# Weight-sum jobs of the pooling layer moved to earlier steps, and rows for the norm loaded ahead of the second half of transposed x

## The chip, the cores and the metric

The kernel runs on one core of one Trainium2 chip. The metric is the device time of one execution in microseconds (us), the median of several executions. Matrix products run on TensorE (PE in the profile), elementwise work on VectorE (DVE), ScalarE (ACT) and GpSimd (POOL); SyncE (SP) issues most loads, POOL issues the stores to DRAM scratch.

## The reference

Two layers, each `h = h + Mixer(rms_norm(h))`, and a norm at the end, for 1024 tokens of width 1024, in fp32. Layer 0 is the pooling mixer, layer 1 stick-breaking attention. The change touches only layer 0:

```python
def pooling_mixer(u, w_in, w_group, scale, w_out):
    proj = u @ w_in                                   # 1024 x 4096
    xb, z = jnp.split(proj, 2, axis=-1)
    xg = xb.reshape(B, S, N_POOL_GROUPS, POOL_GROUP_DIM)
    pooled = jnp.stack(
        [causal_pool_minus_self(xg[:, :, gi], w) for gi, w in enumerate(POOL_WINDOWS)],   # 2, 4, 8, 16
        axis=2)
    mixed = jnp.einsum('bsgi,gio->bsgo', pooled, w_group).reshape(B, S, D_INNER)
    y = mixed * scale * jax.nn.silu(z)
    return y @ w_out
```

## The kernel before

Every product is made of three matmuls in a fast 32-bit type: each operand is split into a high part (ACT, lines 98, 158, 161) and a low part (DVE, lines 99, 159, 162), and high-high, high-low and low-high are added up (`mm3`, lines 89 to 91). A matmul has 512 columns. The first 480 us of the trace are layer 0, the rest is layer 1, which the change leaves alone.

The input projection and the output projection go by a scheme of Strassen's kind: seven products of half blocks in place of eight, for which sums of blocks of the weights and of the activations are formed first.

**The first product (lines 343 to 381).** Tokens are handled in two halves. `c1` is the first product of four blocks of the projection with the one half of transposed x (32 loads and splits in `first_w` and `load_xt`, 96 matmuls), `c2` the same blocks with the other half (`load_xt(k, 1, ...)`, splits into `g4_*` and `g3_*`, 96 matmuls). x isn't scaled for the norm when it is multiplied; the factor is applied afterwards. `factors(l)` (line 176) loads four tiles of rows of x for half `l`, squares and sums them on ACT (line 182) and raises the mean to the power of -1/2 on POOL (184, 185). `spread(l)` (187) has PE copy these factors along the partitions (line 191, four matmuls of 128 columns) and ACT bring them to SBUF (193). `to_u(k, l)` (195) multiplies a tile of x by them on DVE, eight times a half. In `factors` the tiles for the rows come from the two buffers each of `wsum` and `xb`, so the rows for the second half wait until those of the first have been squared.

**The rest of the projection.** `Group(c).rest` (line 244) is what is left of one group of blocks: it loads four blocks of the weights into `a_raw` (6 buffers), has POOL form sums of them (`sums`, lines 221 to 223, and 276), splits blocks and sums (98, 99) and runs 84 matmuls, and DVE brings the products together (214, 250, 260, 266, 269). The order of the blocks is such that the splits of the sums wait for line 223.

**The loop over the four window groups (line 417, `gi`).** In each: two steps `cp`, each a Group (numbers 4 gi and 4 gi + 2) and then `pool_block` for two blocks: sums over the window by repeated adds on DVE (294, two adds for a window of 4, four for 16, on rows of about 1024), 296, 297, and splits into `pl` (302, 303); then two steps `op`, each a Group for the gate (16 + 4 gi, 18 + 4 gi), and `mixed` for two blocks: products of the pooled blocks (PE starts them once all `pl` of the four blocks are there), line 314 on DVE, and POOL stores and differences for the output projection (321 to 338). The first group of both kinds is that of `c1` and `c2`.

**The weight-sum jobs.** The output projection needs sums of blocks of its weights too. `out_sums(kb)` (226) forms those of one of eight parts: four loads on SP into the same `a_raw` buffers, four adds on POOL (221, 222, 223, 231) and four stores that POOL issues (233). The results are read only after the loop. Before, jobs stand after the Group of these steps: 1 at `gi` 0, `op` 1; 2 and 3 at `gi` 1, `op` 0 and 1; 0, 4 and 5 at `gi` 2, `cp` 0, `op` 0 and 1; 7 and 6 at `gi` 3, `cp` 0 and `op` 0.

**What sets the order.** Instructions are emitted in the order of the code; a scheduler places them on each engine by its own timeline, with the release of tile buffers as a constraint, and each engine then works its list in order. A job that is emitted at one step is thus mixed with the sums of the Group behind it, and pool buffers tie the loads to the work that frees them.

Of the kernel before, what the change touches and what calls it, by code (L numbers as in the profile page):

```python
# [9 lines left out]
F32 = mybir.dt.float32  # L10
# [5 lines left out]
P = 128  # L16
S = 1024
D = 1024
DI = 2048
NT = S // P  # L20
NK = D // P
# [24 lines left out]
def trunk(ctx, tc, x, xt, g, pw, pg, psc, pwo, sqk, sv, sz, swo, nf, out):  # L46
# [55 lines left out]
    def raw_of(src, pool, name="w_raw", **kw):  # L102
        raw = pool.tile([P, 512], F32, name=name, **kw)
        nc.sync.dma_start(raw, src)
        return raw
# [31 lines left out]
    def bank():  # L137
        return banks.tile([P, 512], F32, name="bk")

    with tc.tile_pool(name="l0", bufs=2) as l0:  # L140
# [3 lines left out]
        def u_tile(n, kb):  # L144
            t = tuple(l0.tile([P, 512], F32R, name=f"g{n}_{kb}{x_}", bufs=1) for x_ in "hl")
            G[n][kb] = t
            return t

        def pl_tile(dtype=F32):
            return l0.tile([P, 512], dtype, name="pl", bufs=16)  # L150

        def wide(i):
            return l0.tile([P, S + 16], F32, name="xb" if i % 2 else "wsum")

        def split_to(t, raw, scale=None):
            hi, lo = t
            if scale is None:
                act(hi, raw, AF.Copy)
                nc.vector.tensor_tensor(lo, raw, hi, ALU.subtract)
            else:  # L160
                act(hi, raw, AF.Copy, scale=scale)
                nc.vector.scalar_tensor_tensor(lo, in0=raw, scalar=scale, in1=hi, op0=ALU.mult, op1=ALU.subtract)

        def load_xt(k, l, n):


            j, kb = divmod(k, 4)
            t = B[j, l, kb] = pl_tile()
            nc.sync.dma_start(t, xt[k * P:(k + 1) * P, HALVES[l] * 512:HALVES[l] * 512 + 512])
            split_to(u_tile(n, kb), t, g_sb[:, k:k + 1])  # L170
# [5 lines left out]
        def factors(l):  # L176

            ssq = small.tile([P, 4], F32, name="ssq4")
            for j in range(4):
                t = wide(j)[:, :D]  # L180
                nc.sync.dma_start(t, xv[4 * HALVES[l] + j])
                act(t, t, AF.Square, accum_out=ssq[:, j:j + 1])
            rs = rss[l] = small.tile([P, 4], F32, name="rs4")
            nc.gpsimd.tensor_scalar(rs, ssq, 1.0 / D, EPS, ALU.mult, ALU.add)
            nc.gpsimd.tensor_tensor(rs, rs, mhalf.broadcast_to([P, 4]), ALU.pow)

        def spread(l):

            pt = bank()
            for j in range(4):  # L190
                nc.tensor.transpose(pt[:, j * P:(j + 1) * P], rss[l][:, j:j + 1].broadcast_to([P, P]), ident)
            rsb[l] = l0.tile([P, 512], F32, name="w_raw" if l else "rsb", bufs=3 if l else 1)
            act(rsb[l], pt, AF.Copy)
# [7 lines left out]
        def u_split(n, kb, raw):  # L201
            split_to(u_tile(n, kb), raw)
# [15 lines left out]
        def sums(a11, a21, a22):  # L218

            s1 = l0.tile([P, 512], F32, name="w_raw", bufs=3)  # L220
            nc.gpsimd.tensor_tensor(s1, a21, a22, ALU.add)
            nc.gpsimd.tensor_tensor(a21, a21, a11, ALU.add)
            nc.gpsimd.tensor_tensor(a11, a11, s1, ALU.add)
            return s1

        def out_sums(kb):

            a = {(i, j): raw_of(pwo[8 * j + kb][:, i * 512:i * 512 + 512], l0, "a_raw", bufs=6)
                 for i in range(2) for j in range(2)}
            s1 = sums(a[0, 0], a[1, 0], a[1, 1])  # L230
            nc.gpsimd.tensor_tensor(a[0, 1], a[0, 1], a[0, 0], ALU.add)
            for n, t in (5, s1), (7, a[1, 0]), (6, a[0, 0]), (3, a[0, 1]):
                nc.gpsimd.dma_start(wd[n][kb], t)
# [48 lines left out]
        def xb_tile(name="xb", bufs=2):  # L282
            t = l0.tile([P, S + 16], F32, name=name, bufs=bufs)
            nc.gpsimd.memset(t[:, S:], 0.0)
            return t

        def pool_block(gi, c, xb, pooled):
            w = WINDOWS[gi]
            cur, d = xb, 1
            while d < w:  # L290
                nxt = l0.tile([P, S + 16], F32, name="wsum")
                n = S + 16 - 2 * d + 1 if 2 * d < w else S
                n = min(n, S + 16 - d)
                nc.vector.tensor_tensor(nxt[:, :n], cur[:, :n], cur[:, d:d + n], ALU.add)  # L294
                cur, d = nxt, 2 * d
            nc.vector.tensor_tensor(cur[:, S - w + 1:S], cur[:, S - w + 1:S], ratio[w], ALU.mult)
            nc.vector.scalar_tensor_tensor(  # L297
                cur[:, :S], in0=cur[:, :S], scalar=1.0 / w, in1=xb[:, :S], op0=ALU.mult, op1=ALU.subtract)
            for half in range(2):
                cs = slice(half * 512, half * 512 + 512)  # L300
                hi, lo = pooled[c, half] = pl_tile(F32R), pl_tile(F32R)
                act(hi, cur[:, cs], AF.Copy)
                nc.vector.tensor_tensor(lo, cur[:, cs], hi, ALU.subtract)
# [41 lines left out]
        def first_w(j):  # L345
            for a, c in enumerate(first):
                for i in range(2):
                    raw = raw_of(pw[c + i][:, j * 512:j * 512 + 512], l0, "a_raw", bufs=6)
                    n = (7, 5)[a]
                    t = fw[a, i, j] = tuple(  # L350
                        l0.tile([P, 512], F32R, name=f"g{n}_{2 * i + j}{x_}", bufs=1) for x_ in "hl")
                    split_to(t, raw)
                    if j == 0:
                        load_xt(2 * a + i, 0, 1)
                    else:
                        load_xt(4 + 2 * a + i, 0, 2)

        def first_mm(ps, a, i, k, n):
            wh, wl = fw[a, i, k // 4]
            ks = slice(k % 4 * P, k % 4 * P + P)  # L360
            mm3(ps, wh[:, ks], wl[:, ks], *G[n[k // 4]][k % 4], k == 0, k == NK - 1)

        c1 = {(a, i): bank() for a in range(2) for i in range(2)}
        for j in range(2):
            first_w(j)
            for k in range(4 * j, 4 * j + 4):
                for a, i in c1:
                    first_mm(c1[a, i], a, i, k, (1, 2))
        factors(0)
        factors(1)  # L370
        for k in range(NK):
            load_xt(k, 1, (4, 3)[k // 4])
        spread(0)
        c2 = {}
        for a in range(2):
            for i in range(2):
# [12 lines left out]
        for kb in range(4):  # L389
# [5 lines left out]
            dve(B[0, 1, kb], B[0, 0, kb], B[0, 1, kb], ALU.subtract)  # L395
            dve(B[0, 0, kb], t3[kb], B[0, 0, kb], ALU.add)
            u_split(6, kb, B[0, 0, kb])
        firsts = [[xb_tile() for _ in range(2)], [l0.tile([P, S], F32, name="t0") for _ in range(2)]]
        fns = AF.Copy, AF.Silu
        for i in range(2):  # L400
            scaled(firsts[1][i], c1[1, i], 0, fns[1])
# [12 lines left out]
        for kb in range(4):  # L414
            u_split(3, kb, B[1, 1, kb])

        for gi in range(len(WINDOWS)):
            pooled = {}
            for cp in range(2):
                if gi + cp:  # L420
                    dst = [xb_tile("old" if gi == 0 and i else "xb", 2 - (gi == 0 and i)) for i in range(2)]
                    Group(gi * 4 + 2 * cp).rest(dst, AF.Copy)
                    if gi > 1 and cp == 0:
                        out_sums((0, 7)[gi - 2])
                else:
                    dst = firsts[0]
                for i in range(2):
                    pool_block(gi, 2 * cp + i, dst[i], pooled)
            for op in range(2):
                if gi == 3 and op == 1:  # L430

                    y1 = []
                    for kb in range(4):
                        t = wide(kb)
                        raw, hi = t[:, :512], t[:, 512:S].bitcast(F32R)
                        nc.sync.dma_start(raw, yd[1][kb])
                        split_to((hi, raw.bitcast(F32R)), raw)
                        y1.append((hi, raw.bitcast(F32R)))
                if gi + op:
                    dst = [l0.tile([P, S], F32, name="t0") for _ in range(2)]  # L440
                    Group(16 + gi * 4 + 2 * op).rest(dst, AF.Silu)
                else:
                    dst = firsts[1]
                if 0 < 2 * gi + op < 7:
                    out_sums(2 * gi + op)
                for i in range(2):
                    if gi == 3 and op + i == 2:
                        pa = [bank() for _ in range(4)]
                        out_product(pa, lambda kb: (
                            split(raw_of(pwo[kb][:, :512], l0, "a_raw", bufs=6)), y1[kb]), kbs=range(4))  # L450
                    mixed(gi, 2 * op + i, pooled, dst[i])
# [477 lines left out]
```

## Time and profile before

| | us |
|---|---|
| median of three runs | 1605.94 (1605.65 to 1606.53) |
| the profiled execution, its own time | 1603.79 |
| its span in the trace | 1602.1 |
| PE busy | 1545.7 |
| DVE busy | 1135.7 |
| POOL busy | 412.5 |

The span is what the engines' records cover; the execution's own time has 1.7 us around it, and it is 2.1 us under the median. Busy PE time is no measure of the work done: matmuls are pipelined, and at a lower clock one takes longer. What a stretch of the trace did is better read from the number of matmuls in it.

### The profile page before, as it was taken

To read this page: it belongs to the slowest core of one execution; us is meant where nothing else is said; L and a number is where in the kernel's file an instruction comes from. 1 tells how busy PE (TensorE), PEld (TensorE's weight loads), DVE (VectorE), ACT (ScalarE), POOL (GpSimd) and SP (SyncE) were. 2 spreads that over 40 slices of the span, in tenths; PEclk is the share of its full clock that TensorE was granted. 3 is DMA by queue.
4 is the path that set the end of the run, shared out by engine and by line. 5 is a ranking of instruction groups with operands and counts; after the bars stand their busy time and mean duration, and the time that the engine had idled before them with its cause. 6 is when DMAs were issued, how large, how long until landed. Compare 5 with 4: busy or idle time off the path is not lost.

```text
span 1602.1 us, 23391 instructions
## 1 busy us (share of the span) xinstructions
PE 1545.7 (96%) x8256; PEld 1325.5 (83%) x8256; DVE 1135.7 (71%) x1681; ACT 662.8 (41%) x1310; POOL 412.5 (26%) x903
## 2 busy tenths in 40 slices
PE   7899999988989998999999999999999999999997
PEld 6677888866778886989889889889889889889886
DVE  6976957969945676477757757747757757757678
ACT  7432322212335464454435435435434434434444
POOL 0336465586440121111101101101101101101113
PEclk9899999998999998999999999999999999999999
DMA  8124352463468562111021021021021021021112
GB/s 309 33 69 156 105 184 103 149 222 138 147 242 294 183 200 72 56 57 41 27 66 41 27 66 40 27 66 40 28 66 41 27 66 40 28 66 40 33 42 106
DMA packets 75125, 149.92 MB, mean 94 GB/s; under 512 B 9728, under 2 KB 9728, under 8 KB 75008
## 3 DMA queue, kind: packets, MB, share of 16 engines
q1 hardware_dynamic: 67184, 123.25, 23.8%
q0 software_dynamic: 7680, 25.17, 4.2%
q8 instruction: 65, 1.06, 0.3%
q14 instruction: 52, 0.43, 0.1%
q10 hardware_dynamic: 144, 0.01, 0.0%
HBM read 110.64 MB, written 29.36 MB: 87 GB/s over the span
## 4 chain that ended last, share of the span: by engine, by line
PE 72%; DVE 7%; issue 1%; DMA 1%; ACT 1%; POOL 1%; SPq 0%; DVEq 0%; POOLq 0%; ACTq 0%
PE pd L89 15%; PE pd L91 15%; PE pd L90 15%; PE bk L89 4%; PE bk L90 4%; PE bk L91 4%; PE pt L758 4%; PE po L89 2%; PE po L90 2%; PE po L91 2%; PE pq L714 2%; PE pq L715 2%; DVE wsum L294 2%; DVE w_lo L99 1%; DVE wsum L297 1%
## 5 line engine op out<-in xcount | busy, mean ns | idle before, releaser
L726 DVE TENSOR_TENSOR_SCAN om<-om 128x257 f32<-128x257 f32 (+1 forms) x192 | 187.1, 979 | 80.3 <-POOL om L723 34.5
L99 DVE TENSOR_TENSOR w_lo<-w_raw,w_hi 128x512 fp32r<-128x512 f32 x214 | 157.0, 741 | 86.6 <-ACT w_hi L98 82.5
L89 PE MATMUL pd<-slot,w_hi 128*128 128x512 f32 x512 | 202.8, 396 | 4.1 <-DVE slot L542 4.0
L90 PE MATMUL pd<-slot,w_hi 128*128 128x512 f32 x512 | 201.7, 394 | 0.0
L91 PE MATMUL pd<-slot,w_lo 128*128 128x512 f32 x512 | 200.4, 392 | 0.0
L98 ACT ACTIVATE w_hi<-w_raw 128x512 fp32r<-128x512 f32 x214 | 133.6, 627 | 159.8 <-PE pd L90 75.9
L719 ACT ACTIVATE om<-pq 128x256 f32<-128x256 f32 (+1 forms) x192 | 94.4, 492 | 167.7 <-PE pq L715 161.9
L89 PE MATMUL pd<-w_hi,slot 128*128 128x256 f32 x512 | 146.4, 286 | 0.0
L723 POOL TENSOR_SCALAR_AFFINE_SELECT om<-om 128x128 f32<-128x128 f32 x128 | 49.2, 387 | 375.4 <-ACT om L719 373.1
L91 PE MATMUL pd<-w_hi,slot 128*128 128x256 f32 x512 | 144.5, 282 | 0.0
L90 PE MATMUL pd<-w_lo,slot 128*128 128x256 f32 x512 | 144.2, 282 | 0.0
L98 ACT ACTIVATE w_hi<-a_raw 128x512 fp32r<-128x512 f32 x88 | 53.7, 627 | 150.6 <-PE bk L90 57.4
L89 PEld LDWEIGHTS pd<-slot,w_hi 128*128 128x128 f32 x512 | 96.7, 189 | 22.4 <-DVE slot L542 4.3
L762 DVE TENSOR_TENSOR at_l<-pt,at_h 128x512 fp32r<-128x512 f32 (+1 forms) x160 | 99.6, 626 | 21.1 <-ACT at_h L761 20.8
L91 PEld LDWEIGHTS pd<-slot,w_lo 128*128 128x128 f32 x512 | 96.8, 189 | 19.9 <-DVE w_lo L99 0.4
L761 ACT ACTIVATE at_h<-pt 128x512 fp32r<-128x512 f32 (+1 forms) x160 | 86.7, 552 | 63.9 <-PE pt L758 63.2
L90 PEld LDWEIGHTS pd<-slot,w_hi 128*128 128x128 f32 x512 | 96.8, 189 | 18.1
L730 DVE TENSOR_TENSOR om<-pq,om 128x256 f32<-128x256 f32 (+1 forms) x192 | 104.8, 551 | 9.1 <-DVE om L726 0.5
L89 PE MATMUL pd<-w_hi,y_h 128*128 128x512 f32 x256 | 107.0, 418 | 0.4 <-ACT y_h L787 0.4
L90 PE MATMUL pd<-w_lo,y_h 128*128 128x512 f32 x256 | 102.2, 399 | 0.0
L91 PE MATMUL pd<-w_hi,y_l 128*128 128x512 f32 x256 | 100.4, 395 | 0.0
L718 POOL MEMSET om<- 128x1 f32 x192 | 18.0, 99 | 315.2 <-PE pt L758 210.1
(315 smaller groups left out, 4088.7 us busy)
## 6 DMA issues: line engine op xcount, KB each, us to landing
a_raw<-in_pw SPq DMA_DIRECT2D x64, 256.0 KB, 3.3
y_raw<-y_dram SPq DMA_DIRECT2D x52, 256.0 KB, 3.1
y_dram<-t POOLq DMA_DIRECT2D x48, 256.0 KB, 2.9
a_raw<-in_pwo SPq DMA_DIRECT2D x36, 256.0 KB, 2.7
w_raw<-in_sqk SPq DMA_DIRECT2D x34, 256.0 KB, 2.7
w_raw<-in_sz SPq DMA_DIRECT2D x34, 256.0 KB, 3.0
w_raw<-w_dram SPq DMA_DIRECT2D x32, 256.0 KB, 2.9
w_raw<-in_sv SPq DMA_DIRECT2D x32, 256.0 KB, 2.7
```

The lines of the kernel that those rows point to most:

```text
L89: nc.tensor.matmul(ps, lhsT=lh, rhs=rh, start=start, stop=False, skip_group_check=more)
L90: nc.tensor.matmul(ps, lhsT=lh, rhs=rl, start=False, stop=False, skip_group_check=more)
L91: nc.tensor.matmul(ps, lhsT=ll, rhs=rh, start=False, stop=stop, skip_group_check=more)
L98: act(hi, raw, AF.Copy)
L99: nc.vector.tensor_tensor(lo, raw, hi, ALU.subtract)
L719: act(om[:, 1:1 + n], pz, AF.Sigmoid, scale=-ZSCALE)
L723: nc.gpsimd.affine_select(out=om[:, 1:1 + P], in_=om[:, 1:1 + P], pattern=[[1, P]], base=0, channel_multiplier=-1, compare_op=ALU.is_gt, f ...
L726: nc.vector.tensor_tensor_scan(out=om[:, :1 + n], data0=om[:, :1 + n], data1=om[:, :1 + n], initial=1.0 if s.first else carry[r], op0=ALU. ...
L730: nc.vector.tensor_tensor(om[:, :n], pz, om[:, :n], ALU.mult)
L758: nc.tensor.transpose(tp[:, c * P:(c + 1) * P], om[:, (j - b0) * P:(j - b0 + 1) * P], ident)
L761: act(ah[:, :n], tp[:, :n], AF.Copy)
L762: nc.vector.tensor_tensor(al[:, :n], tp[:, :n], ah[:, :n], ALU.subtract)
```

## The change

Two edits. The table `JOBS` places a job after the Group of every `cp` step from the second on, in `gi` 0 to 2: 0 at `gi` 0, `cp` 1; 4 and 5 at `gi` 1, `cp` 0 and 1; 6 and 7 at `gi` 2, `cp` 0 and 1. Jobs 1, 2 and 3 stay where they were, and `gi` 2 `op` and all of `gi` 3 have no job. And both `factors` and the loads of the second half of transposed x are emitted ahead of the second half of `c1`, `spread(0)` inside it, with three of the four tiles of the second half's rows taken from the buffers of `old` and `t0`.

```diff
+        def t0_tile():
+            return l0.tile([P, S], F32, name="t0")
...
             for j in range(4):
-                t = wide(j)[:, :D]
+                if l == 0 or j == 3:
+                    t = wide(j)[:, :D]
+                else:
+                    t = l0.tile([P, S + 16], F32, name="old", bufs=1)[:, :D] if j == 0 else t0_tile()
                 nc.sync.dma_start(t, xv[4 * HALVES[l] + j])
                 act(t, t, AF.Square, accum_out=ssq[:, j:j + 1])
...
         for j in range(2):
             first_w(j)
+            if j:
+                factors(0)
+                factors(1)
+                for k in range(NK):
+                    load_xt(k, 1, (4, 3)[k // 4])
             for k in range(4 * j, 4 * j + 4):
+                if k == 6:
+                    spread(0)
                 for a, i in c1:
                     first_mm(c1[a, i], a, i, k, (1, 2))
-        factors(0)
-        factors(1)
-        for k in range(NK):
-            load_xt(k, 1, (4, 3)[k // 4])
-        spread(0)
...
+        JOBS = {(0, 1): 0, (1, 0): 4, (1, 1): 5, (2, 0): 6, (2, 1): 7}
         for gi in range(len(WINDOWS)):
...
                     Group(gi * 4 + 2 * cp).rest(dst, AF.Copy)
-                    if gi > 1 and cp == 0:
-                        out_sums((0, 7)[gi - 2])
+                    if (gi, cp) in JOBS:
+                        out_sums(JOBS[gi, cp])
...
-                if 0 < 2 * gi + op < 7:
+                if gi == 0 and op or gi == 1:
                     out_sums(2 * gi + op)
```

The lines of the functions named above move down by 3 to 7 (198 becomes 204, 214 becomes 220, 221 to 223 become 227 to 229, 231 and 233 become 237 and 239).

**DVE at the second half of the first product.** `g_0l` to `g_3l` are the low parts of transposed x (first four are `g4`, the next four `g3`), line 198 is `to_u`, line 214 scales a finished product. Before:

```order
L162 SCALAR_TENSOR_TENSOR g_2l<-pl,g_sb,g_2h 128x512
L162 SCALAR_TENSOR_TENSOR g_3l<-pl,g_sb,g_3h 128x512
L162 SCALAR_TENSOR_TENSOR g_0l<-pl,g_sb,g_0h 128x512
L162 SCALAR_TENSOR_TENSOR g_1l<-pl,g_sb,g_1h 128x512
L162 SCALAR_TENSOR_TENSOR g_2l<-pl,g_sb,g_2h 128x512
L162 SCALAR_TENSOR_TENSOR g_3l<-pl,g_sb,g_3h 128x512
L99 TENSOR_TENSOR w_lo<-a_raw,w_hi 128x512
L198 SCALAR_TENSOR_TENSOR pl<-pl,g_sb,rsb 128x512 x8
L214 TENSOR_TENSOR t_571<-bk,rsb 128x512
L214 TENSOR_TENSOR t_572<-bk,rsb 128x512
L214 TENSOR_TENSOR xb<-bk,rsb 128x512 x2
L198 SCALAR_TENSOR_TENSOR pl<-pl,g_sb,w_raw 128x512 x8
```

And now, from the same row `g4_2l` on:

```order
L162 SCALAR_TENSOR_TENSOR g_2l<-pl,g_sb,g_2h 128x512
L204 SCALAR_TENSOR_TENSOR pl<-pl,g_sb,rsb 128x512 x8
L220 TENSOR_TENSOR t_571<-bk,rsb 128x512
L162 SCALAR_TENSOR_TENSOR g_3l<-pl,g_sb,g_3h 128x512
L220 TENSOR_TENSOR t_572<-bk,rsb 128x512
L220 TENSOR_TENSOR xb<-bk,rsb 128x512
L162 SCALAR_TENSOR_TENSOR g_0l<-pl,g_sb,g_0h 128x512
L162 SCALAR_TENSOR_TENSOR g_1l<-pl,g_sb,g_1h 128x512
L162 SCALAR_TENSOR_TENSOR g_2l<-pl,g_sb,g_2h 128x512
L162 SCALAR_TENSOR_TENSOR g_3l<-pl,g_sb,g_3h 128x512
L99 TENSOR_TENSOR w_lo<-a_raw,w_hi 128x512
L220 TENSOR_TENSOR xb<-bk,rsb 128x512
```

The first eight `to_u` now stand ahead of the last five low parts; the second eight follow behind these rows.

**POOL in `gi` 1, at the sums of Group 6 (the second `cp`).** Before, Group 6's sums are those of `w_raw_1355`:

```order
L221 TENSOR_TENSOR w_raw_1355<-a_raw_1351,a_raw_1353 128x512
L276 TENSOR_TENSOR a_raw_1244<-a_raw_1244,a_raw_1160 128x512
L222 TENSOR_TENSOR a_raw_1351<-a_raw_1351,a_raw_1330 128x512
L321 DMA y0_dram_112<-t0_920 128x512
L321 DMA y1_dram_113<-t0_920 128x512
L321 DMA y1_dram_113<-t0_919 128x512
L321 DMA y0_dram_112<-t0_919 128x512
L326 TENSOR_TENSOR t0_920<-t0_920 128x512
L321 DMA y5_dram_117<-t0_920 128x512
L223 TENSOR_TENSOR a_raw_1330<-a_raw_1330,w_raw_1355 128x512
```

Now they are those of `w_raw_1389`, and job 4 (`w_raw_1323`) begins ahead of them:

```order
L228 TENSOR_TENSOR a_raw_1319<-a_raw_1319,a_raw_1315 128x512
L239 DMA w5_dram_121<-w_raw_1323 128x512
L227 TENSOR_TENSOR w_raw_1389<-a_raw_1385,a_raw_1387 128x512
L332 TENSOR_TENSOR t0_936<-t0_936 128x512
L229 TENSOR_TENSOR a_raw_1315<-a_raw_1315,w_raw_1323 128x512
L239 DMA w7_dram_123<-a_raw_1319 128x512
L228 TENSOR_TENSOR a_raw_1385<-a_raw_1385,a_raw_1364 128x512
L327 DMA y5_dram_117<-t0_936 128x512
L237 TENSOR_TENSOR a_raw_1317<-a_raw_1317,a_raw_1315 128x512
L239 DMA w6_dram_122<-a_raw_1315 128x512
L229 TENSOR_TENSOR a_raw_1364<-a_raw_1364,w_raw_1389 128x512
L239 DMA w3_dram_120<-a_raw_1317 128x512
```

All four adds of job 4 and three of its stores stand ahead of line 229 (223 before) of Group 6.

**POOL in `gi` 2, at the sums of Group 24 (the first `op`).** Before, they are those of `w_raw_2362`, behind the last add of Group 10:

```order
L223 TENSOR_TENSOR a_raw_2165<-a_raw_2165,w_raw_2190 128x512
L221 TENSOR_TENSOR w_raw_2362<-a_raw_2358,a_raw_2360 128x512
L276 TENSOR_TENSOR a_raw_2249<-a_raw_2249,a_raw_2165 128x512
L222 TENSOR_TENSOR a_raw_2358<-a_raw_2358,a_raw_2337 128x512
L284 MEMSET xb_2161 128x16
L223 TENSOR_TENSOR a_raw_2337<-a_raw_2337,w_raw_2362 128x512
```

Now they are those of `w_raw_2430`, and job 7 is `w_raw_2362`, whose first add stands one row above these:

```order
L228 TENSOR_TENSOR a_raw_2358<-a_raw_2358,a_raw_2354 128x512
L239 DMA w5_dram_121<-w_raw_2362 128x512
L229 TENSOR_TENSOR a_raw_2354<-a_raw_2354,w_raw_2362 128x512
L239 DMA w7_dram_123<-a_raw_2358 128x512
L227 TENSOR_TENSOR w_raw_2430<-a_raw_2426,a_raw_2428 128x512
L290 MEMSET xb_2212 128x16
L237 TENSOR_TENSOR a_raw_2356<-a_raw_2356,a_raw_2354 128x512
L239 DMA w6_dram_122<-a_raw_2354 128x512
L228 TENSOR_TENSOR a_raw_2426<-a_raw_2426,a_raw_2405 128x512
L239 DMA w3_dram_120<-a_raw_2356 128x512
L290 MEMSET xb_2214 128x16
L229 TENSOR_TENSOR a_raw_2405<-a_raw_2405,w_raw_2430 128x512
```

The whole of job 7, four adds and four stores, is now ahead of the last sum of Group 24.

## Rows read from the trace of the kernel before

**Rows 1.** Windows: busy us and instructions (x) by engine, PE clock, DMA share.

```profile
core 0: us, PE busy (x) PEld busy (x) DVE busy (x) ACT busy (x) POOL busy (x), PEclk, DMA share, GB/s
60.00:80.00 20.00, 16.50 (x62) 12.17 (x60) 20.00 (x31) 9.48 (x17) 6.21 (x2) 0.91 0.09 27
140.00:160.00 20.00, 20.00 (x90) 16.55 (x89) 14.60 (x18) 5.07 (x8) 10.55 (x10) 1.00 0.36 122
160.00:180.00 20.00, 20.00 (x90) 16.56 (x89) 18.90 (x27) 6.63 (x11) 4.33 (x5) 1.00 0.21 71
320.00:440.00 120.00, 103.55 (x430) 82.84 (x429) 100.34 (x106) 30.43 (x53) 79.54 (x76) 0.94 0.49 169
354.40:412.60 58.20, 45.00 (x178) 35.16 (x177) 57.86 (x55) 14.43 (x26) 41.53 (x33) 0.90 0.46 160
```

**Rows 2.** Waits of PE, 0 to 480 us: us in total, times, longest.

```profile
PE bk L89 <- ACT pl L302: 7.7, 3, 4.8
...
PE bk L191 <- POOL rs L185: 5.0, 1, 5.0
...
PE bk L89 <- DVE t L260: 1.6, 1, 1.6
```

**Rows 3.** Timeline, POOL, ACT and PE in `gi` 3: start, us, instruction, [idle before].

```profile
360.07 2.28 POOL L223 TENSOR_TENSOR a_raw<-a_raw,w_raw 128x512 f32<-128x512 f32 x1
362.38 1.15 ACT L98 ACTIVATE w_hi<-a_raw 128x512 fp32r<-128x512 f32 x2 [12.17 <-POOL a_raw L223]
363.06 0.79 PE L89 MATMUL bk<-g_0h,w_hi 128*128 128x512 f32 x1 [7.05 <-ACT w_hi L98]
```

**Rows 4.** Timeline, DVE: the same forms beside a POOL add and without one.

```profile
356.70 2.18 DVE L294 TENSOR_TENSOR wsum<-wsum 128x1037 f32<-128x1037 f32 x1
358.81 0.68 DVE L250 TENSOR_TENSOR avx<-bk,rsb 128x512 f32<-128x512 f32 x1
...
413.27 1.23 DVE L294 TENSOR_TENSOR wsum<-wsum 128x1037 f32<-128x1037 f32 x1
...
268.28 0.69 DVE L303 TENSOR_TENSOR pl<-wsum,pl 128x512 fp32r<-128x512 f32 x1
269.49 1.18 DVE L303 TENSOR_TENSOR pl<-wsum,pl 128x512 fp32r<-128x512 f32 x1
```

**Rows 5.** Timeline at the start: the first instruction of DVE's first and second `to_u`.

```profile
31.70 1.42 DVE L198 SCALAR_TENSOR_TENSOR pl<-pl,g_sb,rsb 128x512 f32<-128x512 f32 x2 [3.57 <-ACT rsb L193]
...
43.27 1.30 DVE L198 SCALAR_TENSOR_TENSOR pl<-pl,g_sb,w_raw 128x512 f32<-128x512 f32 x1 [2.55 <-ACT w_raw L193]
```

**Rows 6.** Timeline, POOL: first and last add of job 6; first and last of `mixed`.

```profile
396.52 1.29 POOL L221 TENSOR_TENSOR w_raw<-a_raw 128x512 f32<-128x512 f32 x1 [2.78 <-DMA a_raw<-in_pwo]
404.10 1.74 POOL L231 TENSOR_TENSOR a_raw<-a_raw 128x512 f32<-128x512 f32 x1
...
354.26 1.30 POOL L333 TENSOR_TENSOR old<-t,old 128x512 f32<-128x512 f32 x1
381.63 1.29 POOL L337 TENSOR_TENSOR t<-old,t 128x512 f32<-128x512 f32 x1
```

**Rows 7.** Timeline in `gi` 1: split of Group 6's sum, and PE's first matmul with it.

```profile
146.36 0.64 ACT L98 ACTIVATE w_hi<-a_raw 128x512 fp32r<-128x512 f32 x1 [2.24 <-PE bk L91]
156.16 0.39 PE L89 MATMUL bk<-g_0h,w_hi 128*128 128x512 f32 x1
```

**Rows 8.** PE at 410 us and 436 us: a window, and the timeline.

```profile
410.00:415.00 5.00, 5.00 (x15) 3.97 (x16) 5.00 (x7) 3.23 (x6) 1.59 (x1) 0.66 0.49 161
436.67 0.47 PE L89 MATMUL bk<-g_0h,w_hi 128*128 128x512 f32 x1 [1.66 <-DVE avx L269]
```

**Rows 9.** Timeline in `gi` 2: sums of Group 24, their split, PE's first matmul with it.

```profile
258.79 2.93 POOL L221 TENSOR_TENSOR w_raw<-a_raw 128x512 f32<-128x512 f32 x1 [7.38 <-DMA a_raw<-in_pw]
270.15 0.63 ACT L98 ACTIVATE w_hi<-a_raw 128x512 fp32r<-128x512 f32 x1 [1.39 <-POOL a_raw L223]
271.63 0.39 PE L89 MATMUL bk<-g_0h,w_hi 128*128 128x512 f32 x1
```

More of the change, by code (lines that the diff above doesn't have):

```diff
@@ L397, in trunk @@
             u_split(6, kb, B[0, 0, kb])
-        firsts = [[xb_tile() for _ in range(2)], [l0.tile([P, S], F32, name="t0") for _ in range(2)]]
+        firsts = [[xb_tile() for _ in range(2)], [t0_tile() for _ in range(2)]]
         fns = AF.Copy, AF.Silu
@@ L439, in trunk @@
                 if gi + op:
-                    dst = [l0.tile([P, S], F32, name="t0") for _ in range(2)]
+                    dst = [t0_tile() for _ in range(2)]
                     Group(16 + gi * 4 + 2 * op).rest(dst, AF.Silu)
```

## The prediction

> **What bounds the kernel now.** I read three views. The windows come first: they say where PE, which does nearly all the work, isn't at its rate. A full stretch of 20 us holds 90 matmuls [rows 1], 0.222 us each. From 320 to 440 us, which is the end of `gi` 2 and `gi` 3, there are 430 where 540 would fit. The list of PE's waits comes next: what it waits for there and before are the splits of the pooled blocks (three times, 7.7 us), the factors of the second `spread` (5.0 us), and a buffer's subtraction (1.6 us) [rows 2]. The timeline is third. In `gi` 3 PE stands 7.05 us because ACT can't split a sum that POOL's line 223 writes only at 362 us [rows 3]. The reader should also see that DVE is busy for 57.86 of the 58.20 us around that place, while POOL is busy for 41.53 [rows 1]: a wait of PE for POOL lies beside a DVE that is never idle, so that taking the wait away gives only what DVE lets it give.
>
> Why DVE is full there stands in its own rows. Line 294 takes 2.18 us beside a POOL add and 1.23 us with none, and line 303 takes 1.18 us and 0.69; line 250, which reads one of its operands from PSUM, takes 0.68 us in the middle of the same adds [rows 4]. So one POOL add costs DVE 0.5 to 1.0 us when it falls into full DVE work. I take 0.9, nearer to line 294, whose forms are the longest part of such a stretch.
>
> The Trainium skill, "SBUF — State Buffer", section "Who interferes with whom", explains the pattern: a VectorE instruction with two SBUF inputs and a GpSimd instruction that reads SBUF lock each other out for a whole instruction, and one with at most one SBUF input doesn't contend. The rows of line 294 and line 250 agree with it. With a whole add of 1.29 us as the price in place of 0.9, the start below would cost 0.8 us more (two adds), `gi` 1 3.1 more (eight), `gi` 3 would give 3.1 more (eight), and the sum would be -3 us in place of -4.
>
> **The change part by part.** It adds no arithmetic: the 8 jobs, the 8 rows and the 16 splits are all still there. What counts is where they fall. Layer 1 is left alone, so that what layer 0 gains or loses by 464 us is the result.
>
> *Start.* PE's wait of 5.0 us for the second factors [rows 2] goes, since the last rows no longer wait for buffers that ACT has to free. In its place DVE now does eight `to_u` before the low part `g4_3l`. Two of them take 1.42 us [rows 5], all eight some 5.5 us from about 31 us on, so the low part comes at about 37 us, and PE, which needs it after ten matmuls (2.2 us), would stand about 4 us. The second eight `to_u` lose the wait of 2.55 us ahead of them, and five low parts and one split are pushed in front (6 of 0.7 us, 4.2), which would make them 1.6 us late; but the first eight begin earlier, since `spread(0)` now stands ahead of the last matmuls of `c1`, and DVE was idle for 3.57 us in front of them [rows 5]. I estimate a start 0 to 0.9 us earlier than 43.27. Then DVE is full, 20.00 of 20 us at 60 to 80, with only two POOL instructions [rows 1], and job 0's four adds now come into about that place. At 0.9 each they cost 3.6 us if all four fall there. Two of them, and the earlier start: **+1 us**, bounds -0.9 and +3.6. Nothing else covers this, for PE waits for the pooled blocks just behind [rows 2].
>
> *`gi` 1.* Jobs 4 and 5 come in. A job holds POOL between 5.2 us (four adds of 1.29) and 9.3 us (from the first add of job 6 to the end of the last, with another add between) [rows 6]; say 7. Job 4 stands ahead of the last sum of Group 6. Now this sum is split at 146.36 and PE takes it up at 156.16, 9.8 us later [rows 7], so a delay by 7 us is covered. What isn't covered is DVE: 8 adds at 0.9 are 7.2 us, while DVE has 5.4 us idle in 140 to 160 and 1.1 us in 160 to 180 [rows 1], and PE is at 90 matmuls in both, that is, at its limit. Some of the idle time is in pieces behind PE. I take **+3 us**; bounds 0 (all of it in the idle time) and +9 (7.2, and 1.7 for a lower clock behind a wait: 5 us at 0.66 in 410 to 415 [rows 8]).
>
> *`gi` 2.* Job 6 takes the place of job 0, which changes nothing. Job 7 is new ahead of the sums of Group 24. Here there is no cover: the split ends at 270.78, PE takes it up at 271.63 [rows 9], 0.85 us later. Job 7's 7 us would make it stand 6.2 us, and a lower clock behind it another 1.7: 7.9 is the upper bound. The lower bound is 0, since POOL was idle for 7.38 us ahead of these sums, waiting for loads [rows 9]; but job 7's four loads now stand in the same SP queue and the same six buffers ahead of those loads. Between ends that far apart I take the middle, **+4 us**. Jobs 4 and 5 leave the `op` steps of `gi` 2, which is no gain in itself, for PE didn't wait there but for the 1.6 us that I count below.
>
> *`gi` 3.* Jobs 7 and 6 go. DVE's full stretch gets shorter by job 6's four adds, 3.6 us; the six operations of lines 333 to 337 that now lie between 354.26 and 381.63 [rows 6] come earlier, as jobs 5 and 7 no longer stand ahead of them on POOL, and I take four of six out of the stretch, 3.6 us. PE's wait of 1.6 us for line 260 [rows 2] goes: its buffer is freed by the POOL work that was behind job 5. So does the wait of 1.66 us at 436.67, and the 5 us at a clock of 0.66 behind 410, 1.7 us [rows 8], where PE and no longer DVE is the limit. 3.6 + 3.6 + 1.6 + 1.7 + 1.7 = 12.2: **-12 us**. The 7.05 us of PE at 363 [rows 3] are no term of their own, since DVE paces that stretch. Bounds: -5 (job 6's adds and the 1.6 alone), and -24 (110 missing matmuls of 0.222 [rows 1], though some of their records may merely be missing).
>
> Sum: 1 + 3 + 4 - 12 = **-4 us**. The profiled execution took 1603.79 us, which would become 1599.8; the median of the runs shown is 2.15 us above it, and -4 from the median is 1602 us. All bounds at their worst give +15.5, at their best -25.
>
> **The rivals.**
> *The wait moves with the jobs (slower).* POOL works in order, and a Group's last sum behind a job is what made PE stand in `gi` 3 [rows 3]. If that comes back in `gi` 2 at its full 7.9 us, and in `gi` 1 at 9, with the start at +1 and the gain at -12, the sum is +6: 1612. For it: 0.85 us of cover in `gi` 2. Against it: 9.8 us in `gi` 1. It ends slower from the point where the two together cost over 14 us.
> *The early jobs are hidden.* If they fall into POOL's and DVE's idle time, `gi` 1 and 2 cost 0, the start gives -0.9 and `gi` 3 -12: -13, 1593. For it: DVE's 6.5 us idle in 140 to 180 [rows 1]. Against it: a PE at its full rate there has no reserve.
> *DVE's load only changes place.* All 32 adds stay. If only the lower bound of `gi` 3 comes, -5, and +1, +2 and +2 before, the sum is 0: 1606.
>
> **Numbers.** The forecast gets 0.43, with a range of its own of 1597 to 1605; the moved wait 0.29; the hidden jobs 0.15; no change 0.13. For 8 in 10 the range goes from the hidden jobs to the moved wait, 1592 to 1612. About 0.2%, 3.2 us, is what a measurement of this kernel can tell from no change. Faster by more than that is three quarters of the forecast and all of the hidden jobs: 0.47. Within it: the rest of the forecast and most of no change, 0.22. Slower: 0.31, the moved wait and a little of no change.
>
> **What would show it.** Start right: PE's wait for line 185 is gone, and one of 3 to 5 us for a low part of line 162 stands at about 33 us. `gi` 1: PE's first wait longer than 2 us, or none, between 150 and 210. `gi` 2: a wait for a split behind line 229 (223 before) at about 272 to 280; if it is over 6 us the moved wait is right. `gi` 3: no wait for a sum at 350 to 370, line 300 (294) with a mean nearer to 1.23 than to 2.18, and layer 0's end some 4 us earlier. The prediction is wrong if DVE stays full for 58 us in `gi` 3 without job 6, or if PE waits in `gi` 1 in spite of its 9.8 us.

## The result and the profile after

The changed kernel takes 1619.59 us (median of four runs, 1618.35 to 1624.86) against 1605.80 for the kernel before: a ratio of 1.0091, with a 95% interval of 1.0069 to 1.0114. It is slower by 13.8 us, 7.6 us above the range of the prediction. A second set of runs gave 1617.62 and 1.0080 (1.0056 to 1.0103). The eight runs of the changed kernel lie within 10.0 us (1614.91 to 1624.86); of the kernel before, 15 runs on one chip lie within 5.2. The profiled execution shown here took 1624.86 us, the slowest of its four; where that matters, the profile of the second set (1618.79 us) stands beside it.

The windows of the changed kernel, with the columns of [rows 1]:

```profile
60.00:80.00 20.00, 15.15 (x59) 11.62 (x57) 20.00 (x25) 8.72 (x15) 11.83 (x9) 0.91 0.36 123
140.00:160.00 20.00, 18.15 (x80) 14.54 (x78) 11.67 (x14) 2.42 (x4) 17.50 (x19) 1.00 0.52 179
160.00:180.00 20.00, 16.83 (x62) 12.94 (x62) 19.93 (x20) 5.76 (x11) 12.95 (x12) 0.83 0.45 152
...
320.00:440.00 120.00, 118.43 (x517) 96.62 (x516) 97.80 (x115) 33.27 (x57) 53.21 (x52) 1.00 0.35 114
```

The gap has moved. From 320 to 440 us PE now runs 517 matmuls in place of 430 (the stages lie up to 20 us later by then, so the work in the two windows isn't the same), but from 140 to 180, where it was at 90 in each 20 us, it runs 80 and 62. DVE is full for 19.93 of 20 us in the second of these, with fewer instructions (20) than the 27 it did there before in 18.90 us.

PE's longest waits in the first 500 us of the changed kernel, to be held against [rows 2] (in us, times, longest):

```profile
PE bk L89 <- DVE xb L266: 11.6, 3, 6.6
PE bk L89 <- ACT y_hi L98: 11.1, 1, 11.1
...
PE bk L89 <- DVE t L220: 4.6, 1, 4.6
PE bk L90 <- DVE g_3l L162: 3.9, 1, 3.9
PE bk L89 <- ACT g_0h L158: 3.5, 1, 3.5
```

The wait at the start for `g_3l` stands where the prediction looked for one. None of the longest is a wait for a sum. DVE's subtractions are late (`xb`, three times, at 183, 298 and 411 us), and 11.1 us come at the first product of the output projection, where before there were 4.30.

A shorter wait does belong to a sum, that of Group 6 behind job 4 in `gi` 1. Before, POOL's line 223 had written it at 146.3 us, and PE took it up 9.8 us later [rows 7]. Now line 229 writes it at 159.4, behind job 4's adds; the rows of before and of now:

```profile
145.05 1.28 POOL L223 TENSOR_TENSOR a_raw<-a_raw,w_raw 128x512 f32<-128x512 f32 x1 [1.32 <-DVE w_lo L99]
```

```profile
157.36 2.08 POOL L229 TENSOR_TENSOR a_raw<-a_raw,w_raw 128x512 f32<-128x512 f32 x1
...
160.16 0.50 PE L89 MATMUL bk<-g_0h,w_hi 128*128 128x512 f32 x1 [2.01 <-ACT w_hi L98]
...
164.14 0.80 PE L91 MATMUL bk<-g_0h,w_lo 128*128 128x512 f32 x1 [2.73 <-DVE w_lo L99]
...
165.00:170.00 5.00, 5.00 (x16) 3.89 (x16) 4.97 (x7) 0.64 (x1) 2.97 (x2) 0.64 0.52 163
```

PE stands 2.01 us at the same matmul, the 561st of the trace, then 2.73 us for the low part, which a full DVE makes late, and after these 4.7 us of standing it runs 16 matmuls in 5 us at a granted clock of 0.64, where it ran 24 at 1.00 before. In the second set the same place has waits of 1.89 and 2.72 us and 13 matmuls at 0.50, the lower of the clock's two levels.

What makes DVE late is seen on its timeline and POOL's: at 203 us, beside job 5, and at 291 us, beside job 7, with PE's wait behind it.

```profile
203.29 6.26 DVE L309 TENSOR_TENSOR pl<-wsum,pl 128x512 fp32r<-128x512 f32 x1
...
202.78 1.31 POOL L229 TENSOR_TENSOR a_raw<-a_raw,w_raw 128x512 f32<-128x512 f32 x1
204.61 1.30 POOL L227 TENSOR_TENSOR w_raw<-a_raw 128x512 f32<-128x512 f32 x1
205.86 1.29 POOL L237 TENSOR_TENSOR a_raw<-a_raw 128x512 f32<-128x512 f32 x1
207.68 1.31 POOL L228 TENSOR_TENSOR a_raw<-a_raw 128x512 f32<-128x512 f32 x1
...
290.94 4.40 DVE L300 TENSOR_TENSOR wsum<-wsum 128x1037 f32<-128x1037 f32 x2
...
298.05 0.79 PE L89 MATMUL bk<-g_0h,w_hi 128*128 128x512 f32 x1 [6.59 <-DVE xb L266]
```

One instruction of 0.69 us (the same form in [rows 4], line 303 there) takes 6.26 us. It begins inside the first of four POOL adds and ends just behind the last; the adds themselves take their 1.3 us. Line 309 at 175.75 us is held for 5.01 us in the same way, through three adds. The second set has the same list of instructions on DVE; there this one is held for 3.18 us only, and PE's wait for `xb` behind it is 0.93 us where it is 3.47 here.

At 291 us two things come together. In the 22 us up to the end of PE's wait DVE's instructions are held for some 6 us in all, and the subtraction that PE stands for comes late by them. And Group 24's last sum, which stands on POOL behind job 7's adds and then waits 2.10 us for DVE's pooling, is written at 298.2 us (before, at 270.1). The product after the one that PE stands for needs it: with an earlier `xb` PE would have run 12 matmuls, 2.7 us, and then stood for the sum. No run here has the one without the other.

Where the time went, stage by stage. The mark is DVE's first scaled product of each `gi` (line 314, then 320), and after it the first matmul of the output projection; in us from the start of the span, and in brackets how much later than before:

| | `gi` 0 | `gi` 1 | `gi` 2 | `gi` 3 | output projection |
|---|---|---|---|---|---|
| before | 115.2 | 201.1 | 310.8 | 427.4 | 468.6 |
| after | 118.6 (+3.3) | 219.0 (+17.9) | 329.1 (+18.3) | 446.8 (+19.5) | 490.4 (+21.8) |
| after, second set | 119.1 (+3.9) | 213.1 (+12.0) | 322.8 (+12.0) | 440.9 (+13.6) | 484.1 (+15.4) |

Behind the last mark the three traces take 1132.7 to 1133.4 us, so layer 0 is the result.

The marks don't have the same work ahead of them: in the changed kernel 44 matmuls fewer are done at the mark of `gi` 2 (1192 for 1236) and 43 more at that of `gi` 3 (1698 for 1655). So here is the same by PE's count, how much later than before its n-th matmul of the trace begins, in us. The 1809th is the first of the output projection.

| | 500th | 600th | 1000th | 1200th | 1700th | 1808th | 1809th |
|---|---|---|---|---|---|---|---|
| before, at | 142.3 | 165.0 | 256.8 | 302.7 | 439.3 | 464.0 | 468.6 |
| after | +1.7 | +9.3 | +19.6 | +28.0 | +8.0 | +14.9 | +21.8 |
| after, second set | +1.9 | +10.1 | +12.4 | +21.7 | +2.3 | +8.8 | +15.4 |

In the second set the place of the late sum (500th to 600th) costs 8.2 us, job 7's stretch (1000th to 1200th) 9.3 us. `gi` 3 then gives 19.4 us back, and 13.1 of these are lost again between the 1700th matmul and the output projection.

### The profile page after: what moved, and what is told of

It is laid out like the page before. It is cut to its first block, busy times and chain, and to the rows that moved or that the text cites. A ratio compares the mean times of both kernels' runs of the same rounds, so it can differ in the third digit from the quotient of the medians.

```text
span 1623.1 us, 23392 instructions
## 1 busy us (share of the span) xinstructions
PE 1552.3 (96%) x8256; PEld 1328.0 (82%) x8256; DVE 1148.3 (71%) x1681; ACT 663.2 (41%) x1310; POOL 406.7 (25%) x903
## 4 chain that ended last, share of the span: by engine, by line
PE 68%; issue 2%; DVE 2%; DMA 1%; POOL 1%; ACT 1%; SPq 0%; DVEq 0%; POOLq 0%; ACTq 0%
PE pd L91 15%; PE pd L89 14%; PE pd L90 14%; PE pt L767 4%; PE bk L89 3%; PE bk L91 3%; PE bk L90 3%; PE po L89 2%; PE po L90 2%; PE po L91 2%; PE pq L723 2%; PE pq L724 2%; DMA y_dram<-old 0%; ACT junk L113 0%; DVE om L735 0%
## 5 line engine op out<-in xcount | busy, mean ns | idle before, releaser
L90 PEld LDWEIGHTS pd<-w_lo,slot 128*128 128x128 f32 x512 | 97.5, 190 | 0.8
```

The lines of the kernel that those rows point to most:

```text
L90: nc.tensor.matmul(ps, lhsT=lh, rhs=rl, start=False, stop=False, skip_group_check=more)
```

## The experiments

Three theories. **HELD**: POOL's adds, moved into stretches in which DVE is full, hold DVE up by more than the 0.9 us each that I took. **LATE**: the sums and loads of the Groups stand behind the jobs in their queues, as in the rival of the moved wait. **START**: the new order of the first product costs the time. Ratios are to runs of the kernel before on the same chip, with a 95% interval.

**e1, the jobs alone; e2, the rows alone.** The kernel before with one half of the change each:

```diff
# e1                                            # e2
+ JOBS = {(0, 1): 0, (1, 0): 4, (1, 1): 5,      + factors(0), factors(1), load_xt(k, 1, ...) at j == 1,
+         (2, 0): 6, (2, 1): 7}                 + spread(0) at k == 6, rows in old and t0
  (table used as in the change)                   (jobs as before)
```

> The kernel before with the table JOBS alone; the start as before. Three theories. HELD: POOL's adds of jobs 4, 5 and 7 hold DVE in its full stretches of gi 1 and gi 2, and PE waits for what DVE is late with. LATE: the same jobs stand ahead of the Groups' last sums on POOL and of their loads on SP, and PE waits for the sums. START: the new order of the first product costs the time. HELD and LATE: the whole loss but for the 2 us that the start cost in the trace of after, 1615 to 1618 us. START: 1602 to 1606.

> The kernel before with the early rows alone, and the jobs where they were. HELD and LATE: 1605 to 1609 us (in the trace of after PE was 2 us behind at 100 us). START: 1615 or more.

Measured: e1 1616.33 us, 1.0070 (1.0054 to 1.0087); e2 1605.14 us, 0.9996 (0.9987 to 1.0005). The whole loss comes with the jobs. The new order of the first product is worth nothing either way, and START falls: in e2 the mark of `gi` 0 lies where it did (115.0 for 115.2), in e1 3.2 us later. So what the start costs is job 0.

**e3, the changed kernel without the adds of jobs 4, 5 and 7**, with their loads and stores where they are:

```diff
 def out_sums(kb):
-    s1 = sums(a[0, 0], a[1, 0], a[1, 1])
-    nc.gpsimd.tensor_tensor(a[0, 1], a[0, 1], a[0, 0], ALU.add)
+    if kb in (4, 5, 7):
+        s1 = a[1, 1]
+    else: (as before)
```

> The kernel after, in which jobs 4, 5 and 7 leave out their four POOL adds and store the raw blocks (12 adds of weights are left out of the computation); their loads, buffers and stores stay in the same queues. HELD: DVE's instructions of over 3 us in gi 1 are gone, and so are PE's waits for line 266 in gi 1 and gi 2; the waits there made up 17 and 9 us, and the time falls by 12 to 20, to 1600 to 1608 us. LATE by loads and buffers: the waits for the sums stay, 1614 to 1619. LATE by the adds' own time on POOL (5 us a job) would lie between, about 1610.

Measured: 1608.48 us, 1.0019 (1.0009 to 1.0028). PE's waits up to 500 us, the longest and what is left of the others at the changed lines:

```profile
PE bk L89 <- ACT y_hi L98: 11.3, 1, 11.3
...
PE bk L89 <- DVE xb L269: 1.5, 1, 1.5
...
PE bk L91 <- DVE w_lo L99: 0.6, 1, 0.6
```

Twelve adds without their loads and stores carry the loss: the first matmul of the output projection comes at 468.8, as in the kernel before, and most of the 2.6 us that are left in the total is a wait in layer 1 (5.90 us in place of 4.03, see e4). LATE by loads and buffers falls, since these are in the queues as in the changed kernel. HELD and LATE by the adds' own time aren't told apart: the time lies just outside HELD's range and under the 1610 of the other. The waits for `xb` fall from 11.6 us to 1.5, and from 100 to 350 us no DVE instruction is longer than 2.6 us. But the last sums of Groups 6 and 24, too, are now written at 151.0 and 275.0 us in place of 159.4 and 298.2, and PE waits for neither. The 11.3 us at the output projection stay: PE arrives there early and stands.

**e4, jobs 4 and 5 back** in the `op` steps of `gi` 2, the rest as changed:

```diff
-JOBS = {(0, 1): 0, (1, 0): 4, (1, 1): 5, (2, 0): 6, (2, 1): 7}
+cp: {(0, 1): 0, (2, 0): 6, (2, 1): 7}, op: {(0, 1): 1, (1, 0): 2, (1, 1): 3, (2, 0): 4, (2, 1): 5}
```

> The kernel after with jobs 4 and 5 back at gi 2, op 0 and 1; 0, 6 and 7 stay where after has them. HELD and LATE: gi 1 loses its 17 us, gi 2 keeps its 9 and gi 3 most of its gain: 1600 to 1608 us. START: 1617 to 1620.

Measured: 1616.29 us, 1.0068 (1.0053 to 1.0083), far above the range of HELD and LATE and just under that of START. By the marks, `gi` 1 now adds nothing (+4.5 at its start and +4.6 at its end, against +3.9 and +12.0): jobs 4 and 5 cost 8.0 us in `gi` 1. At the output projection 5.7 of it are left (478.4 against 484.1). In the total only 1.3 of them show, because layer 1 has a wait of its own, at the same matmul in each kernel, that differs: 5.90 us here at 640.2 us, 2.26 in the changed kernel at 649.1, 4.03 in the kernel before.

**e5, the changed kernel again; e6, job 7 back** at `gi` 3, `cp` 0:

```diff
-JOBS = {(0, 1): 0, (1, 0): 4, (1, 1): 5, (2, 0): 6, (2, 1): 7}
+JOBS = {(0, 1): 0, (1, 0): 4, (1, 1): 5, (2, 0): 6, (3, 0): 7}
```

> The kernel after, unchanged, for a second trace of it: the first was taken of an execution of 1624.86 us, the others took 1618 to 1620. 1617 to 1621 us. HELD: the waits of PE are in the same places (about 160, 183 and 298 us), shorter where no single DVE instruction is held for 5 us.

> The kernel after with job 7 back at gi 3, cp 0; 0, 4, 5 and 6 stay. HELD: PE's wait at 298 us goes with job 7's adds, 9 us, and gi 3 is again as before, 7 us slower in its DVE stretch: 1614 to 1619. If job 7's place in gi 2 costs what I forecast there (4) and gi 3 gave the 12 that I forecast: 1626 to 1630.

Measured: e5 1617.62 us; e6 1610.19 us, 1.0031 (1.0016 to 1.0045), below both ranges. In e5 the waits at 160 and 291 us are as long as in the first trace, and only that at 181, behind the shorter hold, shrinks. Job 7 in `gi` 2 rather than `gi` 3 costs 7.4 us, and 6.4 by the first matmul of the output projection (484.1 to 477.7). With it back in `gi` 3 PE's wait at the output projection is 4.77 us in place of 10.92.

**e7, the kernel before without the adds of jobs 6 and 7**: all that the change could give in `gi` 3, with nothing put elsewhere.

```diff
-    s1 = sums(a[0, 0], a[1, 0], a[1, 1])
-    nc.gpsimd.tensor_tensor(a[0, 1], a[0, 1], a[0, 0], ALU.add)
+    if kb in (6, 7):
+        s1 = a[1, 1]
+    else: (as before)
```

> The kernel before, in which jobs 6 and 7 leave out their four adds (8 adds of weights are left out of the computation); loads, buffers, stores and the order of the jobs stay. It shows what the removal from gi 3 alone is worth. By my forecast's term, 12 us: 1592 to 1596. By the length of gi 3's DVE stretch in the traces, 73 us before and 63 to 66 without jobs, less 2 us in the chain behind it: 5 to 7 us, 1599 to 1601. If the shorter stretch comes from the new order and not from the adds: 1604 to 1607.

Measured: 1605.19 us, 0.9997 (0.9987 to 1.0006). Nothing, where I had forecast 12 us. The time lies in the third range, but not for its reason, since the stretch does get shorter. Its window that answers to the last of [rows 1], and then its timeline at the end of the layer:

```profile
354.40:412.60 58.20, 54.39 (x236) 43.46 (x235) 57.15 (x66) 16.97 (x30) 31.73 (x28) 1.00 0.44 154
```

```profile
443.07 17.14 SPq L334 DMA_DIRECT2D old<-y_dram  x4
460.33 0.39 SPq L104 DMA_DIRECT2D w_raw<-in_pwo  x1
...
466.56 1.65 PE L89 MATMUL bk<-w_hi,y_hi 128*128 128x512 f32 x3 [11.64 <-ACT y_hi L98]
```

In these 58 us PE does 236 matmuls in place of 178, and the wait of [rows 3] is gone. At the 1700th matmul PE is 16.3 us earlier than before, at the last product with the pooled blocks 9.4 us (454.5 for 464.0). Then it stands 11.64 us in place of 4.30, and the gain at the output projection is 2.1 us. At the end there is none; 1.3 us of it go to the wait in layer 1 (5.29 for 4.03). SP is seen in the two rows above: its last four loads of `old` (line 331 before) take from 443.07 to 460.21 to issue, since each waits until POOL is done with the one buffer of `old`. The first loads of the output projection stand behind them.

**e8, jobs 7 and 6 in other steps**, as second jobs at `gi` 1, `op` 1 and at `gi` 2, `op` 1; the rest as before:

```diff
+op: {(0, 1): 1, (1, 0): 2, (1, 1): 3 and 7, (2, 0): 4, (2, 1): 5 and 6}, cp: {(2, 0): 0}
```

> The kernel before with jobs 7 and 6 out of gi 3 and placed as second jobs at gi 1, op 1 and gi 2, op 1, where DVE is idle for 30 to 55% (220 to 260 us, 320 to 340 us of the trace of before). HELD: the adds meet no full DVE, the stretch of gi 3 gets 5 to 7 us shorter, 1599 to 1602. LATE: the second job makes the next Group's sums late, 1606 to 1614.

Measured: 1619.32 us, 1.0078 (1.0061 to 1.0095). Neither range holds it: the `op` steps are no cheaper place for them. By the marks +3.1 at `gi` 2, +14.2 at `gi` 3, +17.2 at the output projection. In the trace PE's longest wait in the loop is 8.19 us at 332.8, for a subtraction into `t` (line 260); DVE stands 12.31 us ahead of it until a store of `t` that POOL issued has landed, and two splits of line 99 after it are held for 4.41 and 4.85 us. So POOL's order and the hold on DVE both appear.

**e9 and e10, the loads of `old` in `gi` 3 issued by POOL**, so that SP's queue holds nothing ahead of the output projection; e9 on the kernel before, e10 on the changed one. **e11** is e9 without the adds of jobs 6 and 7.

```diff
-nc.sync.dma_start(o[:, n * 512:n * 512 + 512], yd[n][kb])
+(nc.gpsimd if gi == 3 else nc.sync).dma_start(o[:, n * 512:n * 512 + 512], yd[n][kb])
```

> The kernel before; in gi 3 the loads into old (line 331) are issued by POOL in place of SP, so that SP's queue holds nothing between the last loads of the layer's own blocks and those of the output projection. QUEUE (PE's wait of 4.3 us at the first product of the output projection comes from loads that stand in SP's queue behind those of old, which wait for POOL): the wait goes, 1601 to 1603 us, ratio about 0.998. CHAIN (the wait is that of the products themselves, DVE's pooling, then mixed, then POOL): the wait stays or comes back a few us later, 1605 to 1607, ratio 1.000.

> The kernel after with the same edit (line 337). QUEUE: PE's wait of 10.9 to 11.1 us at the first product of the output projection goes for the most part, 1608 to 1612 us, ratio 1.002 to 1.004. CHAIN: 1616 to 1620, ratio 1.007 to 1.009, with the wait still over 9 us.

> The kernel before without the four adds each of jobs 6 and 7 (their raw blocks are stored in place of the sums), and with the loads of old in gi 3 issued by POOL. Without the second edit the first gave nothing: PE was 16 us earlier at the end of gi 3 and stood 11.6 us at the output projection. QUEUE: now the 16 us come through for the most part, 1590 to 1596 us, ratio 0.991 to 0.994. CHAIN: 1601 to 1606, ratio 0.998 to 1.000.

Measured: e9 1597.08 us, 0.9952 (0.9939 to 0.9964); e10 1623.75 us, 1.0115 (1.0101 to 1.0129); e11 1596.00 us, 0.9942 (0.9929 to 0.9956). SP and PE at the end of layer 0, in the kernel before and then in e9:

```profile
448.53 13.27 SPq L331 DMA_DIRECT2D old<-y_dram  x4
461.91 0.39 SPq L104 DMA_DIRECT2D w_raw<-in_pwo  x1
...
468.64 1.93 PE L89 MATMUL bk<-w_hi,y_hi 128*128 128x512 f32 x4 [4.30 <-ACT y_hi L98]
```

```profile
451.54 0.45 SPq L104 DMA_DIRECT2D y_raw<-y_dram  x1
...
463.31 1.07 PE L89 MATMUL bk<-w_hi,y_hi 128*128 128x512 f32 x4
```

In the kernel before QUEUE holds: the wait is gone, and the kernel is 8.5 us faster by the medians, below both ranges. The two profiled executions differ by 6.7 us, of which 5.3 are there at the first matmul of the output projection and 1.3 lie in layer 1. In the changed kernel it doesn't hold, and e10 lies above both ranges. There the wait splits in two, 7.01 us at 473.6 for DVE's line 220 and this one:

```profile
496.20 0.69 DVE L99 TENSOR_TENSOR y_lo<-y_raw,y_hi 128x512 fp32r<-128x512 f32 x1 [11.97 <-DMA y_dram<-old]
...
496.95 1.65 PE L91 MATMUL bk<-w_hi,y_lo 128*128 128x512 f32 x3 [9.94 <-DVE y_lo L99]
```

By the trace, DVE's split waits for POOL's last stores of `old`, the same chain by another way. The time of e11 is at the end of QUEUE's range, but e9 alone has nearly all of it. So e11 says that CHAIN is a bound of its own even with the queue clear: PE is 12.7 us earlier than in the kernel before near the end of the layer, then waits 6.81 us for DVE's line 214, and the first matmul of the output projection comes only 2.2 us before that of e9 (461.1, 463.3). In the medians the eight adds are worth 1.1 us, less than can be told from none.

**e12, the opposite move**: e9 with job 0 taken from `gi` 2 into `gi` 3.

```diff
-if gi > 1 and cp == 0:
-    out_sums((0, 7)[gi - 2])
+if gi == 3:
+    out_sums((7, 0)[cp])
```

> The kernel before with the loads of old in gi 3 issued by POOL (1597.1 us) and, in addition, job 0 moved the other way: from gi 2, cp 0 to gi 3, cp 1, so that gi 3 has jobs 7, 0 and 6. PLACE (a job's adds cost about 6 us at the layer's end in gi 1 and gi 2, where the next stage begins later for them, and little in gi 3, where eight adds taken out gave 2.3 us at the first product of the output projection): 6 less in gi 2 and 1 to 3 more in gi 3, 1592 to 1595 us, ratio 0.991 to 0.994. EVEN (a job's adds hold DVE as much in gi 3 as in gi 2): 1596 to 1598, ratio 0.995. ORDER (what job 7 cost in gi 2 was its own place ahead of the sums of Group 24, and job 0's place costs nothing): 1598 to 1603, ratio 0.995 to 0.998.

Measured: 1605.84 us, 1.0000 (0.9991 to 1.0009), that is 8.8 us slower than e9: outside all three. Its waits of PE from 280 to 500 us begin with this row, splits of Groups' sums that POOL writes late:

```profile
PE bk L89 <- ACT w_hi L98: 12.7, 2, 7.3
```

One of the two, 5.32 us at 365, has its counterpart in e9 (8.34 at 364); the other, 7.34 at 398.4, is new, and stands behind job 0's adds. The mark of `gi` 2 lies 1.8 us earlier than in e9 (308.6 for 310.4, with 26 matmuls fewer done), that of `gi` 3 3.0 us later, and the output projection begins 8.5 us later. Eight adds less in `gi` 3 gave nothing, and four more cost 9: by the trace it is LATE's mechanism here.

## Why the prediction was wrong

**The step that failed first is "`gi` 3 ... 12.2: -12 us".** What I counted there happened: no wait for a sum, and a lighter DVE. The forms that answer to each other, of the stretch from the pooling to the first scaled product of `gi` 3, before (354 to 428 us) and after (380 to 447):

```profile
L297 DVE SCALAR_TENSOR_TENSOR wsum<-wsum,xb 128x1024 f32<-128x1024 f32 x4 | 8.7, 2169 | 0.1
L294 DVE TENSOR_TENSOR wsum<-wsum 128x1024 f32<-128x1024 f32 x4 | 8.1, 2028 | 0.0
```

```profile
L300 DVE TENSOR_TENSOR wsum<-wsum 128x1024 f32<-128x1024 f32 x4 | 6.4, 1588 | 0.0
...
L303 DVE SCALAR_TENSOR_TENSOR wsum<-wsum,xb 128x1024 f32<-128x1024 f32 x4 | 5.5, 1376 | 0.0
```

Over all six forms of the pooling (lines 294 to 297, then 300 to 303) it is 39.9 us before and 31.8 after, 8.1 less, against the 7.2 that I had for them (one of the six, the first addition of a block, rose, from 5.9 to 8.6). By PE's count `gi` 3 even gives back more than the 12. But I booked the gain at DVE and PE inside the stretch and didn't follow it to the layer's end. There the last blocks go one after another through line 314, POOL's three operations and the one buffer of `old`, and SP's next loads stand behind that. From the first scaled product to the first matmul of the output projection it is 41.3 us before and 43.6 and 43.2 after: PE's reserve turns into a longer wait (4.30 to 11.1 us). e7 measured the term by itself: 2.1 us at the output projection and 0 in the total; with the queue cleared, e11, 1 us. The 4.30 us at 468 stand in the list of waits from which [rows 2] are taken; I counted what lay ahead of 440 us.

**"I take +3 us" for `gi` 1** was too small: 8.0 us in the second set and by e4, 14.6 in the slower execution shown. Three parts of it failed. First the cover: I took Group 6's sum to be delayed by 7 us and 9.8 us to cover that; it is written 13.1 us later, while PE itself is 1.7 us later there, so the 9.8 are used up, and with the two waits and the lower clock this place costs 7.6 and 8.2 us by PE's count. "PE waits in `gi` 1 in spite of its 9.8 us" was one of the signs of being wrong, and it came. Second, DVE's idle time isn't cover: from 140 to 160 us DVE still had 8.3 us idle, behind PE, while POOL's adds, once begun, ran on into the full stretch behind 160. Third, where a DVE instruction is held through a row of adds, the price of 0.9 us is too low: line 309 loses 6.26 - 0.69 = 5.6 us to four adds, 1.4 each. Over the whole of `gi` 1, though, DVE is busy only 2.8 us longer in the second set and 8.4 in the first (73.3 and 79.0 for 70.6), 0.3 to 1.1 for each of the eight adds. And the row of 0.69 us for line 303 in [rows 4] isn't one without an add: POOL begins one at 268.31, and there it is the add that is longer, 1.81 us.

The Trainium skill ("SBUF — State Buffer", "Who interferes with whom") has a DVE instruction with two SBUF inputs and a POOL instruction that reads SBUF block each other for a whole instruction. By it I had worked out a whole add, 1.29 us, as the other price, and set it aside for 0.9. The 1.4 measured where an instruction is held is nearer to it. Here the trace goes further: the DVE instruction stays blocked through three or four POOL adds in a row, also where a store is issued between two of them.

**`gi` 2, +4 us.** By PE's count job 7's stretch costs 9.3 us in the second set, above my bound of 7.9; of its move 6.4 us are left at the output projection (e6). It isn't the wait that I named: the 6.59 us are one for `xb`, behind held DVE instructions. But Group 24's sum is late too, written just as that wait ends, so that the moved wait stands right behind it.

**The start, +1 us**, measured +3.3 to +3.9, about its upper bound of 3.6. The wait for line 185's factors is gone and the one for `g_3l` is there, 3.90 us where I had said about 4; e2 shows that these two cancel. Job 0 is what is left, 0.8 to 1.0 us for each of its four adds if it is all theirs.

The rival that was nearest, the wait that moves with the jobs, had the right side. It is borne out in `gi` 1, against which it had counted the 9.8 us; in `gi` 2, where it looked for the wait, the sum is late but DVE is what PE stands for. Its sum of +6 also still held the -12.

With the measured terms, at the output projection of the second set: the start 3.9, jobs 4 and 5 5.7 and job 7 6.4 (both net of what they cost in their old places), `gi` 3 between 0 and -2.1 (e7): 14 to 16, against 15.4.

**Still open.** How the hold on DVE and the late sum share the loss behind job 7 in `gi` 2, how the two causes share that of e8, and why the parts of the loss sit in other stages from run to run. The scheduler also places instructions otherwise in each kernel: in the changed one, e7 and e11 24 more matmuls stand ahead of the first product with the pooled blocks of `gi` 3 than in the kernel before. e2 has the same number there and loses nothing, but what the order does to the others wasn't separated. Nor was a second buffer for `old` tried.

## What to carry to other kernels

Follow a gain to the end of its stage: ask what the engine that becomes free will wait for next, and look for loads of the next stage that stand in a queue behind loads which wait for compute; moving eight such loads to another queue gave 8.5 us here, and eight adds less gave nothing. Price work moved onto POOL twice: by what it holds on DVE, up to a whole add each where DVE is full, and by how late it makes what stands behind it in POOL's order (one job with four adds made a sum some 11 us late here, beyond PE's own delay). Don't count DVE's idle time as cover unless it lies at the same moment. A place that loses nothing when work is taken out may still lose when work is put in (e7, e12).

## What the runs showed of the hardware

A DVE instruction with two SBUF inputs can be held through several POOL adds: 6.26 us for one of 0.69, while none of the four adds was longer than 1.31. In other places the two share the delay, 4.40 us for two DVE additions of 1.23 us each, and 1.7 in place of 1.3 us for each of two POOL adds beside them. Where such adds lie in full stretches, the same line is held for a different time in each execution (line 309 at 203 us: 6.26 us in the profile shown; in that of the second set, with the same list of DVE instructions, nothing between 140 and 215 us is longer than 3.18), and the mark of `gi` 1 lies at 219.0 and 213.1 us.
